# Filler work dealt out at two rates beside the RWKV chunks, and an earlier place for the first feed-forward norm

## The chip, the cores and the metric

The kernel runs on one core of a Trainium2 chip. The metric is the device time of one execution in microseconds, taken as the median of several runs. The core has five instruction queues that matter here: TensorE (PE, with its weight loads shown apart as PEld), VectorE (DVE), ScalarE (ACT), GpSimd (POOL) and SyncE (SP, which issues most DMAs). Each queue is worked off in the order in which it was written, so an instruction that waits holds up everything behind it on its engine.

## What is computed

Two layers on one sequence of 1024 tokens with 1024 channels: an RWKV-7 time mixing layer and an mLSTM layer, each followed by a SwiGLU feed-forward layer, each with a modulated RMS norm ahead. The change touches the first layer's mixing and the start of its feed-forward layer.

```python
h = _rms(x) * (1.0 + sc1) + sh1
y = _rwkv7_mix(h, ...)      # six projections of token-shifted inputs, then per head (16 heads of 64):
#   state = state * w_t + (state @ a_t) b_t^T + v_t k_t^T ;  y_t = state @ r_t   (a scan over time)
#   group norm, bonus, gate g, then  @ w_out
x = x + g1 * y
h = _rms(x) * (1.0 + sc2) + sh2
x = x + g2 * _swiglu(h, w_gu, w_down)     # (silu(h @ w_g) * (h @ w_u)) @ w_down
```

## The kernel before, in words

Channels lie on the 128 partitions and tokens on the free axis. The 1024 tokens are worked in two halves of 512 (`hf` 0 and 1). Every float32 matmul of a projection is made of three fast ones (high part times high part and the two mixed terms), so an output tile of 128 channels by 512 tokens from 1024 input channels is 24 matmuls of 512 columns into a PSUM tile named `dn`.

The RWKV scan is done in blocks: a block is one pair of heads (index `j`, 0 to 7) in one half, 16 blocks in all, and a block holds eight chunks of 64 tokens. Each block goes through five stages, and `chunks` runs them as a pipeline over steps `i` from 0 to 18:

- `rw_prep` (block `i`): decays, masked products within a chunk (`sc`, `c1` from `KB`, `AR`), transposes.
- `rw_inverse` (block `i-1`): the inverse of a triangular matrix per chunk, 30 small DVE operations in a row (L676, L678), DMA round trips through DRAM, then small matmuls into `iv`.
- `rw_solve` (block `i-2`): small matmuls into `px` and `tr`.
- `rw_chain` (block `i-3`): the recurrence itself, eight dependent rounds, each PE, then DVE, then PE, then DVE (matmuls named `c<-st,AR`, `c<-VU,SR`, `c<-VU,KT`; DVE L787, L796; ACT L797).
- `rw_finish` (block `i-3`): group norm (ACT L809, L814), transposes `tr<-kc,Ys`, gate, and a store into `yd`.

Beside the blocks stands the filler, a generator (`fillers`) of work that the blocks don't wait for at once: the projections still missing (v of the first half, the gate, then all of the second half: two low-rank ones, k, r, v, gate), then the output projection of the first half (`project`, into the residual tiles `x0`), then the norm of the feed-forward layer on `x0` (`rstd`, `norm_blocks`, and a split of each tile in high and low part), then five calls of `first`, which do part of the feed-forward layer on the first half (48 matmuls of 512 columns each, weights `wgu`). Ahead of each group of projections `mixed` makes the token-shifted input: eight times two ACT and two DVE operations on 128x512.

Each piece yields how much PE work it was, in units of about five matmuls. `chunks` calls `run(limit)` between the stages of a step, and `run` lets the filler go on until its sum reaches the limit, 16 units per step (`QUOTA`). `until` pulls filler ahead when a block needs a projection that isn't made yet. The output projection can't start until eight blocks are finished (`self.finished < 8`).

The order in which this Python code is written is a priority; a scheduler in the language's layer makes the queues' orders from it, by the priorities and by when it thinks that inputs are there. `self.ahead(part)` gives what is recorded inside it a priority that many instructions earlier (`AHEAD`: chain 50, mask 400, finish 50 and so on).

After the last step `phase(FROOM)` closes the block's buffers, and `ffn` begins with `second`: the output projection of the second half (matmuls `c<-ga,wq`, whose inputs `ga` are splits of the loaded `yd` of that half, so the last block must be finished), and splits of the normed first half (`gb<-x`).

## Time and profile before

| | |
|---|---|
| median of 3 runs | 2932.73 us (2917.15 to 2933.27) |
| the profiled execution, its own time | 2919.56 us |
| its span, first to last instruction | 2917.8 us |
| PE busy | 2702.9 us (93%) |
| DVE busy | 2036.1 us (70%) |
| ACT busy | 1401.1 us (48%) |
| mean granted TensorE clock | 0.949 |
| first recurrence (block 0) to start of the feed-forward layer | 267.9 to 1025.8 us |

The span is read in stages by the program's names. A block's turn is taken here from its first `c<-st,AR` matmul to that of the next block; those starts are at 267.9, 318.6, 369.9, 433.8, 479.4, 516.4, 569.0, 610.0, 653.8, 715.5, 754.1, 793.6, 846.4, 883.0, 928.5 and 976.7 us, and the first `c<-ga,wq` is at 1025.8 us. PE's busy share counts pipelined matmuls by their whole length, so that a stretch of small matmuls also looks busy.

### The profile page before, as it was taken

To read this page: it belongs to the slowest core of one execution; us is meant where nothing else is said; L and a number is where in the kernel's file an instruction comes from. 1 tells how busy PE (TensorE), PEld (TensorE's weight loads), DVE (VectorE), ACT (ScalarE), POOL (GpSimd) and SP (SyncE) were. 2 spreads that over 40 slices of the span, in tenths; PEclk is the share of its full clock that TensorE was granted. 3 is DMA by queue.
4 is the path that set the end of the run, shared out by engine and by line. 5 is a ranking of instruction groups with operands and counts; after the bars stand their busy time and mean duration, and the time that the engine had idled before them with its cause. 6 is when DMAs were issued, how large, how long until landed. Compare 5 with 4: busy or idle time off the path is not lost.

```text
span 2917.8 us, 46574 instructions
## 1 busy us (share of the span) xinstructions
PE 2702.9 (93%) x17080; PEld 2124.4 (73%) x17080; DVE 2036.1 (70%) x4029; ACT 1401.1 (48%) x2641; POOL 74.5 (3%) x98
## 2 busy tenths in 40 slices
PE   6899889999898999999999989999989999999988
PEld 5576556677676677887777767778867788887776
DVE  7877776877676468788877677665556865667645
ACT  5766786777666554322244354233435433323433
POOL 0000000000000000000000000000000000000000
PEclk9899789999798999999999989889989999999999
DMA  8775444455543455577788744345264322347734
GB/s 293 262 266 149 121 128 125 119 158 145 155 138 102 134 199 163 187 228 233 243 276 258 229 138 129 121 152 159 94 205 146 106 100 94 107 138 246 237 118 150
DMA packets 359721, 492.38 MB, mean 169 GB/s; under 512 B 125212, under 2 KB 208796, under 8 KB 359492
## 3 DMA queue, kind: packets, MB, share of 16 engines
q1 hardware_dynamic: 345668, 464.24, 50.1%
q10 hardware_dynamic: 13824, 25.17, 2.4%
q8 instruction: 134, 2.20, 0.3%
q14 instruction: 95, 0.78, 0.1%
HBM read 359.77 MB, written 129.50 MB: 168 GB/s over the span
## 4 chain that ended last, share of the span: by engine, by line
PE 61%; DVE 14%; DMA 11%; ACT 6%; issue 6%; POOL 1%; SPq 1%; DVEq 0%; POOLq 0%; ACTq 0%
PE dn L207 23%; PE c L207 20%; PE iv L207 7%; PE px L207 7%; PE sc L207 2%; DMA wraw<-wsd 2%; DMA tt<-gd 1%; DMA wraw<-in_wdn 1%; DVE wq L212 1%; DMA bgs<-in_ada 1%; DVE ga L212 1%; ACT wq L211 1%; DVE wlo L212 1%; PE tr L207 1%; ACT whi L211 1%
## 5 line engine op out<-in xcount | busy, mean ns | idle before, releaser
L207 PE MATMUL dn<-a,whi 128*128 128x512 f32 (+1 forms) x1200 | 434.4, 428 | 20.4 <-ACT a L211 8.0
L211 ACT ACTIVATE wq<-wraw 128x1024 fp32r<-128x1024 f32 x202 | 210.7, 1057 | 335.4 <-DVE wraw L889 89.6
L207 PE MATMUL c<-ga,wq 128*128 128x512 f32 x1446 | 354.2, 394 | 8.6 <-ACT ga L211 7.8
L207 PEld LDWEIGHTS c<-ga,wq 128*128 128x128 f32 x1446 | 271.5, 189 | 73.7 <-ACT ga L211 10.1
L212 DVE TENSOR_TENSOR wq<-wraw,wq 128x1024 fp32r<-128x1024 f32 x202 | 244.3, 1221 | 85.3 <-ACT wq L211 85.1
L207 PEld LDWEIGHTS dn<-a,whi 128*128 128x128 f32 (+1 forms) x1200 | 226.3, 196 | 81.8 <-ACT a L211 10.7
L207 PE MATMUL dn<-a,wlo 128*128 128x512 f32 (+1 forms) x664 | 275.1, 425 | 5.8 <-ACT wlo L443 2.9
L207 PE MATMUL c<-gb,wq 128*128 128x512 f32 x894 | 220.9, 399 | 9.4 <-DVE wq L212 6.4
L207 PEld LDWEIGHTS c<-gb,wq 128*128 128x128 f32 x894 | 169.2, 191 | 49.5 <-DVE wq L212 7.6
L207 PEld LDWEIGHTS dn<-a,wlo 128*128 128x128 f32 (+1 forms) x664 | 128.8, 197 | 37.1 <-issue 4.8
L211 ACT ACTIVATE whi<-wraw 128x1024 fp32r<-128x1024 f32 (+2 forms) x96 | 100.4, 1046 | 113.2 <-PE dn L207 81.9
L212 DVE TENSOR_TENSOR wlo<-wraw,whi 128x1024 fp32r<-128x1024 f32 (+2 forms) x96 | 116.0, 1208 | 45.7 <-ACT whi L211 39.7
L207 PE MATMUL iv<-ga,wq 128*128 128x512 f32 x552 | 136.0, 389 | 0.0
L207 PE MATMUL px<-ga,wq 128*128 128x512 f32 x528 | 128.7, 389 | 0.0
L211 ACT ACTIVATE w<-wraw 128x384 fp32r<-128x384 f32 (+1 forms) x100 | 56.7, 567 | 139.9 <-PE c L207 62.3
L207 PEld LDWEIGHTS iv<-ga,wq 128*128 128x128 f32 x552 | 103.6, 188 | 21.6
L207 PEld LDWEIGHTS px<-ga,wq 128*128 128x128 f32 x528 | 99.1, 188 | 20.7
L207 PE MATMUL dn<-gb,wq 128*128 128x512 f32 x426 | 104.1, 396 | 5.0 <-ACT gb L211 4.7
L207 PE MATMUL iv<-gb,wq 128*128 128x512 f32 x432 | 104.7, 390 | 0.0
L207 PEld LDWEIGHTS dn<-gb,wq 128*128 128x128 f32 x426 | 81.1, 191 | 23.9 <-ACT gb L211 5.3
L207 PE MATMUL c<-ga,w 128*128 128x512 f32 x372 | 93.4, 393 | 1.1 <-DVE ga L212 0.7
L1124 ACT ACTIVATE x<-x 128x512 f32<-128x512 f32 x77 | 48.3, 629 | 95.0 <-DVE x L933 44.9
(607 smaller groups left out, 5643.5 us busy)
## 6 DMA issues: line engine op xcount, KB each, us to landing
wraw<-in_wgu SPq DMA_DIRECT2D x110, 512.0 KB, 3.5
tt<-gd SPq DMA_DIRECT2D x154, 256.0 KB, 4.1
KT<-in_ada SPq DMA_DIRECT2D x40, 512.0 KB, 5.3
gd<-x SPq DMA_DIRECT2D x77, 256.0 KB, 2.0
gd<-tt SPq DMA_DIRECT2D x72, 256.0 KB, 2.1
wraw<-wsd SPq DMA_DIRECT2D x32, 512.0 KB, 4.7
bgs<-in_ada SPq DMA_DIRECT2D x96, 128.0 KB, 3.3
wraw<-in_wdn SPq DMA_DIRECT2D x24, 512.0 KB, 4.4
```

The lines of the kernel that those rows point to most:

```text
L207: return self.nc.tensor.matmul(out, lhsT, rhs, start=start, stop=stop, **kw)
L211: self.nc.scalar.activation(hi, src, AF.Copy)
L212: self.nc.vector.tensor_tensor(lo, src, hi.bitcast(F32), SUB)
L1124: nc.scalar.activation(t, t, AF.Silu)
```

## The change

`QUOTA` becomes two rates: 19.6 units per step up to step 11 and 12.6 after it, so that the sum at the end of step 18 is 316.4 units where it was 304. The filler has 317. And the norm of the first half with its splits is recorded inside `ahead("front")` with 400.

```diff
-QUOTA = 16
+
+QUOTA = 19.6, 12.6
-AHEAD = dict(chain=50, mask=400, w=50, finish=50, pair=100, g=150, norm=500)
+AHEAD = dict(chain=50, mask=400, w=50, finish=50, pair=100, g=150, norm=500, front=400)
...
         self.store(0, x0)
-        self.norm_blocks(x0, 0, self.rstd(x0))
-        hp = []
-        for x in x0:
-            hi, lo = self.a0()
-            self.split(hi, lo, x)
-            hp.append((hi, lo))
+        with self.ahead("front"):
+            self.norm_blocks(x0, 0, self.rstd(x0))
+            hp = []
+            for x in x0:
+                hi, lo = self.a0()
+                self.split(hi, lo, x)
+                hp.append((hi, lo))
...
+        def quota(x):
+            return QUOTA[0] * min(x, 11) + QUOTA[1] * max(x - 11, 0)
...
-            run(QUOTA * (i + POS[0]))
+            run(quota(i + POS[0]))
...
-            run(QUOTA * (i + 1))
+            run(quota(i + 1))
```

No instruction is added or taken away on any engine; the queues' orders change. Counted on PE in both built programs, the filler's matmuls of 512 columns between one block's first recurrence matmul and the next block's are:

| block | 0 | 1 | 2 | 3 | 4 | 5 | 6 | 7 | 8 | 9 | 10 | 11 | 12 | 13 | 14 | 15, to the feed-forward layer |
|---|---|---|---|---|---|---|---|---|---|---|---|---|---|---|---|---|
| before | 68 | 40 | 89 | 71 | 51 | 93 | 72 | 93 | 135 | 68 | 17 | 86 | 63 | 26 | 110 | 130 |
| after | 65 | 116 | 96 | 72 | 96 | 96 | 96 | 96 | 32 | 96 | 49 | 95 | 57 | 87 | 48 | 0 |

Ahead of block 0's recurrence stand 15 more than before.

Three places show it. Line numbers of the changed kernel are one or two higher up to `rw_finish`. The first place is PE around the norm's matmuls (`sc<-kc,mt` sums the squares, `sc<-kc,rs` spreads the result). Before, they stand in block 13's recurrence, with block 14's solve (`tr<-kc,ld`, `px<-VU,SA`) between:

```order
L207 MATMUL c_302_1589<-st_1582,AR_9163 128x128
L207 MATMUL sc_10670<-kc,mt_10647 128x1 x4
L742 MATMUL tr_10566<-kc,ld_10563 128x128 x3
L207 MATMUL c_302_1589<-VU_10024,SR_9175 64x64 x2
L207 MATMUL c_302_1589<-VU_10024,KT_9220 64x64 x2
L742 MATMUL tr_10566<-kc,ld_10563 128x128
L207 MATMUL px_10582<-VU_10565,SA_9795 64x64
L207 MATMUL sc_10678<-kc,rs_10675 128x128
L207 MATMUL c_302_1589<-st_1582,AR_9163 128x128
L207 MATMUL sc_10678<-kc,rs_10675 128x128
```

The next filler matmul comes 30 rows further down, after the inverse and the solve of block 14 and the first round of its recurrence. In the changed kernel the same matmuls stand at the end of block 11's recurrence, right behind the last matmul of the output projection (`dn_9723`):

```order
L208 MATMUL dn_9723<-a_8329,wlo_9720 128x512
L208 MATMUL c_302_1589<-VU_9134,SR_8397 64x64 x2
L208 MATMUL c_302_1589<-VU_9134,KT_8442 64x64 x2
L208 MATMUL c_302_1589<-st_1582,AR_8385 128x128
L208 MATMUL sc_9955<-kc,mt_9932 128x1 x4
L208 MATMUL c_302_1589<-VU_9134,SR_8397 64x64 x2
L208 MATMUL c_302_1589<-VU_9134,KT_8442 64x64 x2
L208 MATMUL sc_9963<-kc,rs_9960 128x128 x4
L208 MATMUL iv_9297<-XN_9284,SA_8937 16x16 x32
L208 MATMUL dn_10022<-a_9984,whi_10018 128x512
```

Two blocks earlier, and with one matmul row of block 12's inverse before the first `first` matmul (`dn_10022`).

The second place is PE at the end of the last block. Before, filler stands between the last transposes (`tr<-kc,Ys`) and 22 more behind them:

```order
L817 MATMUL tr_11522<-kc,Ys_11356 128x128
L207 MATMUL dn_11544<-a_10723,whi_11539 128x512
L207 MATMUL dn_11544<-a_10724,whi_11539 128x512
L207 MATMUL dn_11544<-a_10723,wlo_11540 128x512
L817 MATMUL tr_11522<-kc,Ys_11356 128x128
```

In the changed kernel the last filler matmul stands ahead of block 15's inverse; its solve, recurrence and transposes have none beside them, and `c<-ga,wq` of the feed-forward layer follows the transposes at once:

```order
L208 MATMUL c_302_1589<-VU_11243,SR_10647 64x64 x2
L208 MATMUL c_302_1589<-VU_11243,KT_10692 64x64 x2
L818 MATMUL tr_11599<-kc,Ys_11433 128x128 x4
L208 MATMUL c_1919_11735<-ga_11692,wq_11732 128x512 x3
L208 MATMUL c_1919_11735<-ga_11697,wq_11732 128x512 x3
```

149 filler matmuls stood behind the start of that inverse before, none now. The third place is ACT at the same point. Before, the last block's scaling (`Ys<-Ys`) is followed by the filler's rest, a weight split (`wq`) and splits `gb<-x`, and then the split `ga<-tt` that the first matmul needs:

```order
L814 ACTIVATE Ys_11356<-Ys_11356,gm_11498,gv_11499 128x64 x8
L978 ACTIVATE tmp_11572<-tmp_11572 128x512
L971 ACTIVATE mt_11594<-dn_11580 128x512
L211 ACTIVATE wq_11732<-wraw_11730 128x1024
L211 ACTIVATE gb_11978<-x_9249 128x512
L211 ACTIVATE gb_11981<-x_9251 128x512
L211 ACTIVATE gb_11984<-x_9253 128x512
L211 ACTIVATE gb_11987<-x_9255 128x512
L211 ACTIVATE ga_11692<-tt_11690 128x512
```

Now the eight `gb` splits stand among the squares (`gj`) of the last block's norm, five `wq` splits stand earlier still, and `ga<-tt` comes right behind the scaling:

```order
L810 ACTIVATE gj_11577,gv_11576<-Ys_11433,gm_11575 128x64
L212 ACTIVATE gb_11996<-x_8281 128x512
L810 ACTIVATE gj_11577,gv_11576<-Ys_11433,gm_11575 128x64
L212 ACTIVATE gb_11999<-x_8283 128x512
L810 ACTIVATE gj_11577,gv_11576<-Ys_11433,gm_11575 128x64 x3
L815 ACTIVATE Ys_11433<-Ys_11433,gm_11575,gv_11576 128x64 x8
L212 ACTIVATE ga_11692<-tt_11690 128x512
```

## Rows read from the trace of the kernel before

**Rows 1.** The page: PE's part of section 1, the clock of section 2 (40 slices)

```profile
PE 2702.9 (93%) x17080; PEld 2124.4 (73%) x17080; DVE 2036.1 (70%) x4029; ACT 1401.1 (48%) x2641; POOL 74.5 (3%) x98
PEclk9899789999798999999999989889989999999999
```

**Rows 2.** Busy time in stretches, all instructions; behind the engines: granted clock, DMA share, GB/s

```profile
267.90:1025.80 757.90, 682.27 (x7647) 494.87 (x7646) 541.76 (x1394) 519.62 (x1249) 33.51 (x30) 0.91 0.46 134
267.90:433.80 165.90, 139.07 (x1483) 95.06 (x1482) 125.67 (x325) 129.38 (x277) 3.99 (x5) 0.85 0.44 127
754.10:793.60 39.50, 33.89 (x440) 25.52 (x441) 24.11 (x57) 25.63 (x71) 1.75 (x2) 0.70 0.50 161
846.40:883.00 36.60, 36.27 (x489) 26.92 (x487) 29.05 (x74) 20.53 (x50) 2.12 (x2) 1.00 0.50 134
```

**Rows 3.** Blocks 3 to 15, filler (tile dn) alone: length, PE, PEld, DVE, ACT, clock

```profile
433.80:479.40 45.60, 20.90 (x71) 12.76 (x71) 0.00 (x0) 4.14 (x8) 0.93 0.42 127
479.40:516.40 37.00, 15.28 (x51) 8.73 (x51) 0.00 (x0) 2.64 (x5) 1.00 0.47 131
516.40:569.00 52.60, 29.58 (x94) 16.66 (x93) 0.00 (x0) 2.08 (x4) 0.94 0.40 114
569.00:610.00 41.00, 21.16 (x72) 12.62 (x72) 0.00 (x0) 1.34 (x3) 1.00 0.53 150
610.00:653.80 43.80, 26.63 (x93) 16.14 (x93) 0.00 (x0) 2.34 (x4) 1.00 0.56 162
653.80:715.50 61.70, 36.56 (x135) 24.12 (x135) 0.00 (x0) 3.53 (x6) 1.00 0.51 139
715.50:754.10 38.60, 23.91 (x69) 12.19 (x68) 0.00 (x0) 4.64 (x8) 0.91 0.57 161
754.10:793.60 39.50, 5.79 (x17) 3.02 (x17) 0.00 (x0) 1.17 (x2) 0.70 0.50 161
793.60:846.40 52.80, 26.62 (x87) 15.59 (x86) 2.98 (x4) 0.00 (x0) 0.90 0.46 135
846.40:883.00 36.60, 18.13 (x63) 10.92 (x63) 1.49 (x2) 0.00 (x0) 1.00 0.50 134
883.00:928.50 45.50, 7.57 (x26) 4.66 (x26) 1.48 (x2) 0.00 (x0) 0.77 0.41 118
928.50:976.70 48.20, 33.07 (x110) 20.39 (x110) 2.75 (x4) 2.39 (x4) 0.93 0.35 104
976.70:1026.00 49.30, 35.01 (x131) 23.08 (x130) 4.14 (x6) 3.54 (x6) 0.96 0.42 142
```

**Rows 4.** Timeline of PE: three filler matmuls, start us, length of all, operation

```profile
1016.34 0.39 PE L207 MATMUL dn<-a,wlo 128*128 128x512 f32 x1
1016.57 0.62 PE L207 MATMUL dn<-a,whi 128*128 128x512 f32 x2
1017.02 0.39 PE L207 MATMUL dn<-a,wlo 128*128 128x512 f32 x1
```

**Rows 5.** Timeline of PE: last projection matmul, norm's sums, first `first` matmul

```profile
894.53 0.40 PE L207 MATMUL dn<-a,wlo 128*128 128x512 f32 x1
...
904.67 0.95 PE L207 MATMUL sc<-kc,mt 128*128 128x1 f32 x8
...
930.80 0.79 PE L207 MATMUL dn<-a,whi 128*128 128x512 f32 x1 [0.57 <-ACT a L211]
```

**Rows 6.** Stretches without filler, all instructions, columns as in rows 2

```profile
756.20:780.10 23.90, 19.68 (x271) 14.48 (x269) 15.21 (x34) 15.76 (x50) 1.75 (x2) 0.50 0.40 134
```

**Rows 7.** Timeline of all engines at the end of the last block

```profile
1011.21 0.33 PE L817 MATMUL tr<-kc,Ys 128*128 128x128 f32 x1 [1.50 <-ACT Ys L814]
...
1022.12 1.06 ACT L211 ACTIVATE wq<-wraw 128x1024 fp32r<-128x1024 f32 x1 [5.43 <-DMA wraw<-in_wro]
...
1023.08 2.17 ACT L211 ACTIVATE gb<-x 128x512 fp32r<-128x512 f32 x4
...
1025.82 0.79 PE L207 MATMUL c<-ga,wq 128*128 128x512 f32 x1 [7.05 <-ACT ga L211]
```

More of the change, by code (lines that the diff above doesn't have):

```diff
@@ L1481, in chunks @@
                 self.rw_solve(S[i - 2])
-            run(QUOTA * (i + POS[1]))
+            run(quota(i + POS[1]))
             if 1 <= i < 17:
                 self.rw_inverse(S[i - 1])
-            run(QUOTA * (i + POS[2]))
+            run(quota(i + POS[2]))
             if i < 16:
```

## The prediction

> **What bounds the kernel now.** I read the page first, then the busy times of stretches, then the filler alone block by block, then PE's timeline where the filler stops. PE is busy for 93% of the span [rows 1], but that share says little in the chunk stage, where small matmuls count as busy too. The change touches only the orders of that stage, 267.9 to 1025.8 us. There PE is busy 682.3 of 757.9 us at a mean clock of 0.91, DVE 541.8 (71%) and ACT 519.6 (69%) [rows 2]: no engine is full, each waits for the others in turn. The clock has two levels, 1.2 and 2.4 GHz; a mean of 0.91 means that about 18% of the stage, 136 us, ran at the lower one.
>
> What a block's turn costs shows in the filler rows [rows 3]. Full-rate filler matmuls start 0.23 us apart: from 1016.34 to 1017.02 us are three steps [rows 4]. Five turns are smooth: 72 filler matmuls in 41.0 us, 93 in 43.8, 69 in 38.6, 63 in 36.6, 110 in 48.2. They lie within 1.5 us of one line, 23 us + 0.23 us per matmul (39.6, 44.4, 38.9, 37.5, 48.3). Below some 63 matmuls the line stops: 51 took 37.0 us and 17 took 39.5. So a turn has a floor of about 38 us, set by the block's own rounds over PE, DVE and ACT, and under it filler costs nothing. Five other turns lie above: 71 in 45.6 (+6.3), 94 in 52.6 (+8.0), 135 in 61.7 (+7.7), 87 in 52.8 (+9.8), 26 in 45.5 (+7.5 over the floor), 39 us together. They are turns in which `mixed` or the norm loads ACT and DVE, or the clock was low (0.93, 0.94, 0.90, 0.77).
>
> The first three blocks are another case: 165.9 us [rows 2] for 197 filler matmuls (68 + 40 + 89 in the table), where the line would give 3 x 23 + 197 x 0.23 = 114 us. ACT is busy 129.4 us (78%) and DVE 125.7 (76%) [rows 2]: `mixed` and the low-rank projections load these two there, and PE waits for them.
>
> **The change part by part.** No instruction is added or removed, and no DMA; every term is a move, and the filler counts per block in the table of the section on the change carry the sum.
>
> Start: 15 more filler matmuls ahead of block 0's recurrence, 15 x 0.23 = 3.4 us, so 267.9 becomes 271.3 us.
>
> Blocks 0 and 1: they now take 181 matmuls, nearly the work that three blocks took before (197), and it is the same stretch of filler. DVE then needs 125.7 us less one block's own DVE work. That work is about 24 us: block 10's turn, with 17 filler matmuls, has 24.1 us of DVE and 25.6 of ACT [rows 2]. So DVE needs 101 us and ACT 129.4 - 22 = 107 us (22 between block 10's 25.6 and block 12's 20.5 [rows 2]). At the shares reached before, 76% and 78%, that is 133 and 137 us; at 86 and 90%, the most I would grant, 118. I take 130. The price by the line alone, 38 + 49.7 = 88 us, is the lower bound, if only PE counted.
>
> Blocks 2 to 14 by the line: six turns of 96 matmuls at 45.1 us (270.6), one of 72 (39.6), one of 95 (44.9), one of 87 (43.0), and four at the floor (32, 49, 57, 48 matmuls: 152). Together 550.1 us.
>
> What lies above the line: three sets of `mixed` (for r, v and the gate) remain, at the mean of 7.9 us of the five turns above, 24 us. The norm remains as well. Before, PE had no filler from 894.9 to 930.8 us, 36 us, because `first` waits for the norm [rows 5]; but block 13's recurrence and block 14's inverse and solve ran in it, so that turn was only 7.5 us over the floor. In the changed order the norm's matmuls stand right behind the last projection matmul, and just two rounds of the recurrence and one part of an inverse stand before the first `first` matmul. The chain itself is not shorter than its parts: from the last projection matmul to the first sum it took 9.8 us (894.9 to 904.7), from there to the first `first` matmul 26.1 us [rows 5], with other work between on ACT and DVE. With priority I estimate half of this 36 us, 18 us, of which the little work beside it covers some 10. So the priority makes the gap shorter but also takes its cover away: 8 us over the line, as before. In all 24 + 8 = 32 us; bounds 15 (the low clock does not come back) and 40 (as before).
>
> Block 15's recurrence so starts at 271.3 + 130 + 550.1 + 32 = 983.4 us, where it was 976.7.
>
> The end: before, 131 filler matmuls lay in the 49.3 us from that start to the feed-forward layer [rows 3]. None are left, so their 30 us of PE work are paid for in the sums above. From the start to the first transposes it was 34.5 us (976.7 to 1011.2), and from there 14.6 us to the first `c<-ga,wq` [rows 7]. The recurrence's rounds are dependent and don't get shorter without filler. The eight `gb` splits now stand among the last block's squares on ACT: 8 x 0.54 us = 4.3 us [rows 7], of which some 3 delay the last norm. In return the weight and input splits that stood behind the transposes are done by then, and only the scaling's end, one `ga` split and its DVE half are left: about 3 us instead of 14.6. So the end takes 34.5 + 3 + 3 = 40.5 us (37 to 47), and the feed-forward layer starts at 1023.9 us instead of 1025.8.
>
> The sum is -1.9 us against the profiled execution's 2919.56 us, thus about 2918. The three runs' median is 13 us above that execution, and one of the runs (2917) is below it; the mean of the four is 2925.7. I put the time at 2925.7 - 2 = 2924 and forecast no change that can be measured, which for this kernel means within 1%, 29 us.
>
> A rule weighed against rows: from 756.2 to 780.1 us, with almost no filler, PE ran at a clock of 0.50, though small matmuls kept it busy 19.7 of 23.9 us [rows 6]. That turn took 39.5 us, and block 12's at full clock 36.6 [rows 3], so 24 us at the lower level cost at most 3 us there: the rounds wait for DVE and ACT anyway. The Trainium skill ("TensorE: Matmul & The Clock Gate", sections Terms and HAM oscillation) prices throttled time at half of it and tells that gaps in TensorE's work bring the low clock back. By that rule the same stretch would have cost 12 us, and the sum would come out about 68 us lower if the changed order kept the clock up for all of the 136 us.
>
> **The rivals.**
> *The early blocks take their filler at PE's price.* Then blocks 0 and 1 cost 88 us and not 130, and the time is about 2924 - 42 = 2882 us. For it: neither ACT nor DVE is full there. Against it: the same filler kept them at 78 and 76% for three blocks [rows 2], as high as in engines that work in a fixed order and wait for each other anywhere in this stage. Even half of it would give 2903.
> *The bare end decides, and the kernel gets slower.* The 149 matmuls that stood behind the start of block 15's inverse cost 149 x 0.23 = 34.3 us where they now stand, if the earlier turns have no room under the floor; the end gives back 8.8 us. That is +25 us, about 2950. For it: six turns of 96 matmuls lie well above the floor, where each matmul has its full price. Against it: two long turns with 17 and 26 matmuls [rows 3] had room for some 80. It decides once more than three of the turns 2 to 9 take over 50 us.
> *Even filler keeps the clock up.* The low clock goes with turns of little filler (0.70, 0.77), and most turns over 60 matmuls ran at 0.9 to 1.0 [rows 3]. If the 32 us above the line fall away, and a part of the time in the first blocks (clock 0.85 [rows 2]), the time is 2924 - 32 = 2892, at most 2880. Against it: the longest low stretch lay where nothing waited for PE [rows 6], so it had cost little. By the Trainium skill's rule named above this case would be the likeliest.
> *The priority does nothing.* `first` still waits for the whole norm, and ACT makes its inputs at 1.3 us per three matmuls of 0.7 us. Then nothing is gained or lost by that edit: 2924 all the same.
>
> **How the numbers follow.** Forecast (with the last rival, which has the same time) 0.50, its own range 2908 to 2940 from the bounds 118 and 137 for the first blocks, 15 and 40 above the line, 37 and 47 at the end, which I don't add up in one direction. Early blocks cheaper 0.17, clock kept up 0.13, bare end 0.20. The range reaches to the other cases, 2884 to 2954. Faster by more than 1%, under 2903 against the median, takes most of the two cheaper cases, 0.25; slower by more than 1%, over 2962, only the bare end together with a bad turn or two, 0.07; the rest is 0.68. That is about what a measurement of this kernel can tell from no change.
>
> **What the changed profile would show.** Right: blocks 0 and 1 together 118 to 137 us with ACT and DVE near 80%; turns of 96 matmuls at 44 to 50 us; no turn under 36 us; block 15's start between 970 and 995 us, and the first `c<-ga,wq` 37 to 47 us behind it with PE at the low clock between; the norm's gap in filler half as long. Wrong: blocks 0 and 1 under 110 us, or turns of 96 matmuls over 50 us, or a first `c<-ga,wq` more than 15 us off 1024 us. From there on both kernels run the same orders, and the spans behind that point should agree within a few us.

## The result and the profile after

The changed kernel is slower: 2953.35 us against 2926.97 us (medians of six runs each), ratio 1.0103 (95% interval 1.008 to 1.0126; it is taken over all runs, the medians alone give 1.009). Its profiled execution took 2953.41 us, its span is 2951.6 us (2917.8 before), so 33.8 us have to be found. Some 7 of them are chance: the profiled execution of the kernel before (2919.56 us) is a short one, 7 to 12 us under the medians of that kernel beside all runs here (2926 to 2932 us). Every comparison of traces below has this in it. The page's PE line and clock line, which answer [rows 1]:

```profile
PE 2706.0 (92%) x17080; PEld 2128.7 (72%) x17080; DVE 2037.2 (69%) x4029; ACT 1408.8 (48%) x2645; POOL 72.3 (2%) x98
PEclk9899889999979789999999998998989999999999
```

The work is the same on every engine, within 8 us. The stretches of the chunk stage, against [rows 2] (columns as there): the whole stage, turns 0 and 1, turns 0 to 2, turns 3 to 14, and the end.

```profile
275.50:1047.60 772.10, 675.73 (x7616) 491.61 (x7615) 546.74 (x1392) 529.53 (x1258) 31.41 (x30) 0.90 0.46 133
275.50:411.80 136.30, 110.08 (x1030) 73.75 (x1028) 99.84 (x236) 106.83 (x208) 1.87 (x3) 0.85 0.44 128
275.50:464.80 189.30, 160.17 (x1554) 109.61 (x1553) 132.85 (x323) 141.40 (x303) 5.25 (x6) 0.86 0.43 125
464.80:1008.10 543.30, 498.74 (x5977) 370.93 (x5975) 396.65 (x1032) 371.53 (x906) 23.34 (x23) 0.94 0.49 140
1008.10:1047.60 39.50, 16.82 (x90) 11.07 (x89) 17.24 (x37) 16.59 (x52) 2.81 (x2) 0.50 0.22 75
```

Turns 0 to 2 take 189.3 us instead of 165.9; turns 3 to 14 take 543.3 us, and 542.9 before (433.8 to 976.7); the end takes 39.5 instead of 49.1. The filler alone for the turns that matter (turns 1, 2, 4, 9, 10, 11, 13; columns as in [rows 3], where turns 4 to 13 of before stand):

```profile
327.80:411.80 84.00, 43.93 (x116) 23.24 (x116) 0.00 (x0) 10.91 (x17) 0.82 0.42 124
411.80:464.80 53.00, 28.10 (x96) 17.24 (x96) 0.00 (x0) 4.66 (x8) 0.90 0.40 117
...
508.10:553.50 45.40, 26.73 (x96) 16.88 (x96) 0.00 (x0) 2.82 (x5) 1.00 0.55 157
...
725.10:778.00 52.90, 27.85 (x96) 17.91 (x96) 2.24 (x3) 0.54 (x1) 0.94 0.58 173
778.00:813.40 35.40, 16.65 (x50) 8.82 (x49) 2.25 (x3) 0.00 (x0) 0.95 0.47 120
813.40:883.80 70.40, 30.15 (x95) 18.99 (x95) 2.18 (x3) 1.16 (x2) 0.78 0.32 93
...
919.90:967.50 47.60, 25.64 (x88) 14.96 (x87) 2.03 (x3) 2.40 (x4) 1.00 0.45 132
```

Turn 4 stands for four with 96 matmuls, at 44.6 to 45.9 us. The long ones are turn 1 (84.0 us) and turn 11 (70.4 us), which holds the norm. PE's timeline there, against [rows 5]: last projection matmul, sums, one row of block 12's inverse, first `first` matmul. Below it DVE in the same stretch.

```profile
846.50 0.40 PE L208 MATMUL dn<-a,wlo 128*128 128x512 f32 x1
...
849.73 1.05 PE L208 MATMUL sc<-kc,mt 128*128 128x1 f32 x8 [0.55 <-DVE mt L331]
...
857.72 0.72 PE L208 MATMUL iv<-XN,SA 16*16 16x16 f32 x64 [3.52 <-DVE XN L696]
859.17 0.79 PE L208 MATMUL dn<-a,whi 128*128 128x512 f32 x1 [0.72 <-ACT a L212]
```

```profile
851.65 0.35 DVE L797 SCALAR_TENSOR_TENSOR st<-st,dl,c 128x128 f32<-128x128 f32 x1 [0.67 <-PE c L208]
...
854.24 3.08 DVE L862 TENSOR_TENSOR x<-x,sc 128x512 f32<-128x512 f32 x5 [1.22 <-PE sc L208]
857.23 0.43 DVE L696 STREAM_TRANSPOSE XN<-XD 128x256 f32<-128x256 f32 x1
```

The gap in filler shrank from 36 us to 12.3 us (846.9 to 859.2), as the priority was to do. But the turn is 25.6 us over the prediction's line (23 us + 0.23 us per matmul), twice the gap, so the gap alone doesn't make it. Block 11's last round ends on DVE at 852.0 us (L797). Behind it stand five of the norm's eight operations (L862), and only then the transpose (L696) that block 12's inverse waits for. So the matmuls of this inverse begin only when the recurrence is over: the transpose comes 43.8 us into the turn, and the next recurrence starts 26.6 us behind it; in turns 4 to 7 the same transpose came 11 to 27 us into the turn, beside the recurrence. How much of the 25.6 us this order makes is not shown.

The end, against [rows 7]: PE at the last transposes and the first `c<-ga,wq`, SP and ACT at the loads between.

```profile
1042.79 0.47 PE L818 MATMUL tr<-kc,Ys 128*128 128x128 f32 x1 [10.97 <-ACT Ys L815]
...
1047.24 3.76 SPq L1505 DMA_DIRECT2D ga<-in_xT  x8
1047.60 5.95 PE L208 MATMUL c<-ga,wq 128*128 128x512 f32 x15 [2.34 <-ACT ga L212]
...
1051.10 1.86 SPq L834 DMA_DIRECT2D tt<-yd  x3
1058.10 1.93 ACT L212 ACTIVATE ga<-tt 128x512 fp32r<-128x512 f32 x3 [7.95 <-DMA tt<-yd]
...
1058.79 3.65 PE L208 MATMUL c<-ga,wq 128*128 128x512 f32 x7 [5.23 <-ACT ga L212]
```

PE waits 11.0 us for the last block's scaling; that costs nothing against the kernel before, where filler ran in this time (the first transpose stands 34.7 us behind block 15's start, 34.5 before). It waits 2.3 us at the first `c<-ga,wq`, and 5.2 us more after 15 of them: the last three loads of `yd` stand on SP behind eight loads of `in_xT` that were issued from 1047.24 on. Before, those eight were issued from 1017.1 to 1024.7 us, ahead of the first `c<-ga,wq` at 1025.8, and PE then went through these matmuls with waits under 0.3 us:

```profile
1020.69 2.83 SPq L1500 DMA_DIRECT2D ga<-in_xT  x6
...
1026.86 1.52 SPq L833 DMA_DIRECT2D tt<-yd  x3
...
1026.89 13.62 PE L207 MATMUL c<-ga,wq 128*128 128x512 f32 x47 [0.27 <-DVE ga L212]
```

So the three loads of `yd` start 3.5 us behind the first `c<-ga,wq`, where it was 1.0 us, and they take 7.0 us to land, where it was 5.2. The feed-forward layer's later matmuls `c<-gb,wq` therefore start 53.3 us behind the first `c<-ga,wq`, where it was 47.2 (columns: start, length of all, operation; before, then after):

```profile
1072.99 2.20 PE L207 MATMUL c<-gb,wq 128*128 128x512 f32 x9
```

```profile
1100.87 2.43 PE L208 MATMUL c<-gb,wq 128*128 128x512 f32 x10
```

The sum of the 33.8 us: block 0's start +7.6, turns 0 to 2 +23.3, turns 3 to 14 +0.5, the end -9.7, the start of the feed-forward layer +6.1, all behind it +5.9. That last part varies by itself: 1842.6 to 1857.7 us over the 20 kernels run here, with the kernel before third from below (1844.8). Why block 0 starts 7.6 us later is not shown.

### The profile page after: what moved, and what is told of

Its sections match the earlier page's. It is cut to its first block, busy times and chain, and to the rows that moved or that the text cites. A ratio compares the mean times of both kernels' runs of the same rounds, so it can differ in the third digit from the quotient of the medians.

```text
span 2951.6 us, 46587 instructions
## 1 busy us (share of the span) xinstructions
PE 2706.0 (92%) x17080; PEld 2128.7 (72%) x17080; DVE 2037.2 (69%) x4029; ACT 1408.8 (48%) x2645; POOL 72.3 (2%) x98
## 4 chain that ended last, share of the span: by engine, by line
PE 39%; DMA 9%; DVE 8%; issue 5%; ACT 2%; SPq 1%; POOL 1%; DVEq 0%; POOLq 0%; ACTq 0%
PE c L208 14%; PE dn L208 13%; PE iv L208 6%; PE px L208 4%; DMA wraw<-in_wdn 2%; DMA wraw<-wsd 2%; DMA bgs<-in_ada 2%; DMA tt<-gd 2%; DVE wq L213 1%; PE sc L208 1%; ACT wq L212 1%; DVE ga L213 1%; DMA tt<-yd 1%; DMA wsd<-bgs 0%; DMA bgs<-in_wdn 0%
## 5 line engine op out<-in xcount | busy, mean ns | idle before, releaser
L208 PE MATMUL dn<-a,whi 128*128 128x512 f32 (+1 forms) x1200 | 435.7, 431 | 24.1 <-ACT a L212 12.5
L208 PE MATMUL dn<-a,wlo 128*128 128x512 f32 (+2 forms) x664 | 278.8, 430 | 6.9 <-DVE wlo L478 4.2
L208 PEld LDWEIGHTS c<-gb,wq 128*128 128x128 f32 x894 | 170.6, 193 | 46.1 <-DVE wq L213 7.3
L208 PEld LDWEIGHTS dn<-a,wlo 128*128 128x128 f32 (+2 forms) x664 | 131.3, 200 | 39.6 <-issue 6.5
L208 PEld LDWEIGHTS iv<-gb,wq 128*128 128x128 f32 x432 | 81.3, 188 | 17.3 <-DVE x L934 0.3
```

The costliest lines, as they stand in the source:

```text
L208: return self.nc.tensor.matmul(out, lhsT, rhs, start=start, stop=stop, **kw)
```

## The experiments

All edits are against the changed kernel, but for e5_light_before, which is made from the kernel before; ratios are to the kernel before on the same chip. "Bare end" means that next to no filler is left behind block 15's start; a "covered" end has it.

**Each half of the change alone.** e1_rates keeps the two rates, without the priority:

```diff
-AHEAD = dict(chain=50, mask=400, w=50, finish=50, pair=100, g=150, norm=500, front=400)
+AHEAD = dict(chain=50, mask=400, w=50, finish=50, pair=100, g=150, norm=500)
```

> The two rates alone, the norm at its old priority. The filler counts per block are those of the changed kernel but for blocks 12 and 13 (48 and 96 for 57 and 87), and no filler stands at the end. Theory A (the bare end): the rates cost nearly all, so about 2950 us, as the changed kernel. Theory B (the norm's priority takes the cover off its gap: block 11's turn took 70.4 us where the line gives 44.9): the turn with the norm falls by some 15 us, so about 2938 us.

Measured 1.0049 (1.0029 to 1.0069). That is half of the loss: less than the first theory had forecast, more than the second. Turns 0 to 2 take 192.4 us and the end is bare, as in the changed kernel; the one turn that differs by much is the norm's, 60.9 us instead of 70.4 (turns 13 and 14 differ too, but take 87.7 and 88.2 us together). DVE in that turn of e1_rates:

```profile
851.96 1.87 DVE L862 TENSOR_TENSOR x<-x,sc 128x512 f32<-128x512 f32 x3
...
856.04 0.44 DVE L696 STREAM_TRANSPOSE XN<-XD 128x256 f32<-128x256 f32 x1
```

Here too the norm's operations, all eight, stand ahead of the transpose, which comes 40.9 us into the turn; so that order comes with the rates, not with the priority. What the priority changes here is the cover: without it the gap is 17.7 us long and five of the recurrence's eight rounds begin in it, with it 12.3 us and one round. The 47 filler matmuls ahead of the gap then take 33.5 us instead of 17.7, and the 48 behind it 24.6 instead of 25.4.

e2_front keeps the priority, at 16 units a step; e12_front_again is the same kernel with more rounds:

```diff
-QUOTA = 19.6, 12.6
+QUOTA = 16, 16
```

> One rate of 16 as before, the norm at priority 400. 136 filler matmuls remain behind block 15's start (130 before). Theory A: the end is as before, so no slower than the kernel before; the turns 13 and 14 with 77 and 56 matmuls in place of 26 and 110 save some 8 us by the line, so 2915 to 2927 us. Theory B: the gap of the norm costs 25 us over the line as in the changed kernel's block 11, so about 2940 us.

> The priority of the norm alone with 16 units a step, the same kernel as in an earlier run (which gave 0.9977), with more rounds to narrow the interval. If the priority by itself brings something, the ratio stays at 0.996 to 0.999; if that was chance, it lies at 1.000 to 1.002.

Measured 0.9977 (0.9957 to 0.9997) and 0.9981 (0.9959 to 1.0002): a gain of some 0.2%, which the first of the two intervals sets apart from none and the second doesn't. So the rates make the kernel slower, and the priority adds some 0.5% to it, while at 16 units, where the norm falls into turn 13, it adds nothing. That it is the many filler matmuls in the norm's turn that make the difference is likely and not shown.

**Other rates.** e3_end gives the filler a flat rate, without the priority, that leaves 51 matmuls behind block 15's start. e4_18 has 18 units and then 12.5, with 136 left there; e8_18_old_norm is the same without the priority; e7_front16_15 has 16 and then 15 with the priority, and 145 left.

```diff
-QUOTA = 19.6, 12.6
+QUOTA = 16.65, 16.65    # e3_end, without front
+QUOTA = 18, 12.5        # e4_18; e8_18_old_norm without front
+QUOTA = 16, 15          # e7_front16_15
```

> One rate of 16.65, whose sum at the last step is that of the changed kernel (316), and the norm at its old priority. Blocks 0 and 1 have 56 and 40 matmuls, as few as before; behind block 15's start stand 51 in place of 130. Theory A: the 79 matmuls gone from the end cost 79 x 0.23 = 18 us, less some 5 us by which the end gets shorter, so about 2940 us. Theory C (the 181 matmuls pressed into blocks 0 and 1 are what costs, 10 us and more): about 2927 us, as before.

> Rates 18 and 12.5 (sum 298 in place of 316), the norm at priority 400 as in the changed kernel. 136 matmuls remain behind block 15's start, and only one turn of 2 to 14 has less than 50. Theory A: the end is paid for again, and by the line of 23 us and 0.23 us per matmul the turns 0 to 14 take 605 us where before they take 624, so about 2908 us, faster than both. Theory B: the norm's gap adds 17 us to that, so about 2925 us. Theory C: blocks 0 and 1 with 130 matmuls cost some 5 us over before.

> Rates 18 and 12.5 as in the fourth run (2970 us), but the norm at its old priority; the counts per block are nearly the same (52 and 52 for 57 and 47 at the end). If the priority made the 45 us gap in filler at the norm there, the gap shrinks and the time falls to about 2945 us; if the rate of 18 puts filler in lumps by itself (a 41 us gap in block 4 and 5, far from the norm), it stays at about 2965 us.

> Rates 16 and 15 with the norm at priority 400: 145 filler matmuls behind block 15's start in place of 130, and turns 13 and 14 with 71 and 65 in place of 26 and 110. Theory A: 15 matmuls more are free at the end (3 us) and the even turns save 8 us, about 2918 us, faster than both kernels by little. If the end is already full, about 2925 us.

Measured: e3_end 1.0057 (1.0041 to 1.0073), e4_18 1.0143 (1.0126 to 1.016), e8_18_old_norm 1.0133 (1.0101 to 1.0166), e7_front16_15 0.9985 (0.9968 to 1.0002). e3_end, with nearly the old first blocks (173.6 us) and without the priority, still loses. Its end and its start of the feed-forward layer, to `c<-gb,wq`, take 96.3 us together, as before, so that 79 matmuls less bring nothing there; turns 0 to 14 take 719.6 us instead of 708.8. e4_18 and e8_18_old_norm are the slowest of all, and that with a covered end (2908 to 2925 us had been forecast for e4_18, 2971 came), so a bare end isn't the only way to lose. In e4_18 filler stops for two long stretches (columns as in [rows 3]):

```profile
521.00:562.00 41.00, 0.03 (x1) 0.00 (x0) 0.00 (x0) 1.08 (x2) 0.63 0.44 113
912.00:957.00 45.00, 0.34 (x2) 0.00 (x0) 0.75 (x1) 0.00 (x0) 0.56 0.37 98
```

The second is the norm's gap. What holds the filler back in the first I did not settle.

**Filler left out at the end.** e6_light_after and e5_light_before compute less: three `first` calls take two of their eight input tiles, 108 filler matmuls less. In the changed kernel these stood in turns 13 and 14, in the kernel before behind block 15's start.

```diff
-            self.product(pa, (hi[:, :HT], lo[:, :HT]), hp[:4])
+            few = 1 if l == 0 and n in (2, 3, 4) else 4
+            self.product(pa, (hi[:, :HT], lo[:, :HT]), hp[:few])
...
-            self.product(pb, (hi[:, HT:], lo[:, HT:]), hp[4:])
+            self.product(pb, (hi[:, HT:], lo[:, HT:]), hp[4:4 + few])
```

> The kernel before, with three of the five early `first` calls (n = 2, 3, 4) summing over a quarter of the input channels: 108 filler matmuls are left out, and 103 of them are missing behind block 15's start (27 left of 130). Its result is so not the layer's. Theory A (the end's length is that of the last block's own chain and the feed-forward layer's start, so filler there is free): no change, 2920 to 2932 us. If filler has its price everywhere: 108 x 0.23 = 25 us less, about 2905 us.

> The changed kernel with the same 108 matmuls left out of the same three calls. There they are missing from the turns of blocks 13 and 14 (23 and 1 left of 87 and 48), none from the end, which has none. Theory A: these turns fall to the floor of about 38 us each, 12 us less, and up to 25 us less if the floor is lower: about 2930 to 2940 us against some 2953 us. If the changed kernel's extra time does not come from the filler's place: no change.

Measured 1.0031 (1.0011 to 1.005) and 1.0121 (1.0086 to 1.0155): no gain from less work in either. In e5_light_before the end and the start of the feed-forward layer take 98.5 us together with 103 matmuls less, 96.3 with them: in the kernel before, filler at the end is free. In e6_light_after turns 13 and 14, with 23 matmuls and 1, take 91.6 us; in the changed kernel, with 87 and 48, 88.2. The filler of these two turns alone, columns as in [rows 3]:

```profile
917.50:974.60 57.10, 9.14 (x24) 4.40 (x23) 2.75 (x4) 2.37 (x4) 0.67 0.44 128
974.60:1009.10 34.50, 0.72 (x2) 0.19 (x1) 0.68 (x1) 0.60 (x1) 0.64 0.45 134
```

The granted clock falls to 0.67 and 0.64, where it was 1.00 and 0.83: about 49 us more at the lower level. Two readings remain: the rounds set the length of these turns, or what was saved in matmuls (108 x 0.23 = 25 us) went into the lower clock. The Trainium skill ("TensorE: Matmul & The Clock Gate", sections Terms and HAM oscillation) prices throttled time at half; by this, as an estimate, 24 of the 49 us, which would fit the second. No run here has these turns light and at full clock, so it stays open. For the kernel both mean the same: filler is free in these two turns.

**First blocks or bare end?** The decomposition above pointed to turns 0 to 2. e9_late has the old rate up to step 6 and the changed kernel's sum from step 11 on, so only the bare end and the priority are left of the change; e10_early has the early rate and then falls back to the old line, without the priority, so only the first blocks are left.

```diff
-            return QUOTA[0] * min(x, 11) + QUOTA[1] * max(x - 11, 0)
+            return 16 * x if x < 6 else (96 + (215.6 - 96) / 5 * (x - 6) if x < 11 else 215.6 + 12.6 * (x - 11))      # e9_late
+            return 19.6 * x if x < 6 else (117.6 + (160 - 117.6) / 4 * (x - 6) if x < 10 else 16 * x)                 # e10_early
```

> The changed kernel with another sum of filler by step: 16 units a step up to step 6 as in the kernel before, then faster, so that from step 11 on the sum is the changed kernel's. Filler matmuls per block: 68 40 89 95 72 144 120 120 32 96 52 92 58 96 38, and none behind the start of block 15's inverse; 681 done by the start of block 3's recurrence as before (776 in the changed kernel). Theory 'the price is paid in the first blocks, where ACT and DVE are loaded': block 3's recurrence starts at 434 us (464.8 in the changed kernel), the middle turns stay near 543 us together whatever filler they hold (three of them with 120 to 144 may add up to 15), and the time is 2922 to 2940 us, though the end is as bare as in the changed kernel. Theory 'the bare end decides': the end has no filler, so the start of the feed-forward layer is no earlier than 1045 us and the time stays at 2945 to 2955 us.

> The kernel before (no priority for the norm, 16 units a step at the end) with 19.6 units a step up to step 6 and then fewer until the sum is back on its line at step 10. Filler matmuls per block: 65 116 96 51 88 50 99 65 82 53 13 74 63 90 56, and 136 behind block 15's start (before 130); 776 done by the start of block 3's recurrence, as in the changed kernel. Theory 'the price is paid in the first blocks': block 3's recurrence starts at about 465 us instead of 433.8, the 95 matmuls less in the turns behind it give little back, and the time is 2945 to 2962 us with an end as full as before. Theory 'the bare end decides': the end is that of the kernel before, so the time is within 6 us of it.

Measured: e9_late 1.0117 (1.008 to 1.0153), e10_early 1.0039 (1.0015 to 1.0062). That overturned the theory that the price is paid in the first blocks alone: with them as before, e9_late (2965.6 us) is as slow as the changed kernel, and slower than either theory had forecast for it. The filler alone in turns 0 to 2, turns 3 to 14 and the end (columns as in [rows 3]): before, e9_late, e10_early.

```profile
267.90:433.80 165.90, 73.36 (x198) 37.24 (x197) 0.00 (x0) 19.82 (x32) 0.85 0.44 127
433.80:976.70 542.90, 265.21 (x885) 157.78 (x885) 8.71 (x12) 24.29 (x42) 0.92 0.47 135
976.70:1025.80 49.10, 35.01 (x131) 23.08 (x130) 4.14 (x6) 3.54 (x6) 0.97 0.41 141
```

```profile
266.50:437.50 171.00, 77.79 (x198) 39.62 (x197) 0.00 (x0) 19.48 (x31) 0.79 0.43 123
437.50:1012.20 574.70, 300.49 (x1015) 181.21 (x1015) 12.84 (x18) 28.06 (x48) 0.94 0.48 138
1012.20:1052.30 40.10, 0.00 (x0) 0.00 (x0) 0.00 (x0) 0.00 (x0) 0.50 0.27 89
```

```profile
282.10:474.20 192.10, 98.63 (x278) 54.55 (x277) 0.00 (x0) 24.12 (x39) 0.84 0.42 123
474.20:1005.80 531.60, 246.48 (x785) 141.76 (x784) 8.74 (x12) 19.95 (x34) 0.89 0.46 132
1005.80:1057.80 52.00, 37.30 (x137) 24.13 (x136) 4.14 (x6) 3.59 (x6) 0.97 0.40 135
```

In e9_late the 130 matmuls that the end lost cost 31.8 us in turns 3 to 14, 0.245 us each, and the end gave back 9.0. (Its profiled run is 16 us below its median.) In e10_early turns 0 to 2 cost 26 us more and turns 3 to 14 give back 11. (Its profiled run is 19 us above its median.) So the first blocks alone explain some 11 of the 26 us in the medians, and the end's filler spread over turns 3 to 14, with the priority, can explain all. A bare end with neither the priority nor the early rate was not run; e3_end, with 51 matmuls left, comes nearest and loses 0.6%.

**The price by place.** Three kernels leave 105 filler matmuls out of the changed kernel, with all operations of the other engines kept: in turns 1 and 2 (e13_light_1_2), in turns 5 to 7 (e14_light_5_7), 67 ahead of block 0 and 38 in turn 0 (e15_light_0). In e14_light_5_7 all other turns hold the same filler within one matmul; in e13_light_1_2 turns 10 to 14 divide the same sum in another way (92, 52, 59, 105 and 28 matmuls), and in e15_light_0 some turns differ by up to 6.

```diff
-            self.dense(ps, wt, xs)
+            self.dense(ps, wt, xs[:1] if hf == 1 and arr == "k" and j < 5 else xs)   # e13; e14: "v"; e15: hf == 0, "v", j > 2
```

> The changed kernel with 105 filler matmuls left out of the second half's k projection (five of its eight output tiles take one input tile of eight, so k is not the true one there). Turn 1 then has 53 filler matmuls instead of 116 and turn 2 has 54 instead of 96; all operations on DVE, ACT and the DMAs stay. The turns from 10 on hold the same sum with another division. Theory 'ACT and DVE bind the first blocks': turns 0 to 2 stay at 185 to 189 us and the time is within 6 us of the changed kernel's, a ratio to before of 1.008 to 1.013. Theory 'every filler matmul costs PE's price of 0.23 to 0.24 us there': block 3's recurrence starts 24 us earlier, at about 441 us, and the ratio is 1.000 to 1.004.

> The changed kernel with 105 filler matmuls left out of the second half's v projection (five of its eight output tiles take one input tile of eight, so v is not the true one there). Turns 5, 6 and 7 have 53, 74 and 56 filler matmuls instead of 96 each; all other turns have the same as in the changed kernel. By the prediction's line (23 us and 0.23 us per matmul, floor 38) these turns go from 45 to 38, 40 and 38 us: block 15's recurrence starts 19 us earlier, at 989 us, ratio 1.003 to 1.007. Theory 'the rounds of the blocks set these turns at 45 us whatever the filler': nothing changes, 1.008 to 1.013.

> The changed kernel with 105 filler matmuls left out of the first half's v projection (five of its eight output tiles take one input tile of eight, so v is not the true one there): 67 of them ahead of block 0's recurrence, 38 in turn 0, which keeps 27. Theory 'ACT and DVE bind the first blocks': block 0's recurrence starts up to 15 us earlier, if PE bounds the stretch ahead of it, and turn 0 stays near 52 us. Theory 'PE's price': both together 24 us earlier. If neither, the ratio stays at 1.010.

Measured: 1.0019 (1.0002 to 1.0035), 1.0061 (1.0037 to 1.0085) and 0.9995 (0.9974 to 1.0016). Against the changed kernel's 1.0103 that is some 25, 12 and 32 us. Turn 1 of e13_light_1_2, the filler alone (columns as in [rows 3]) and then all instructions (columns as in [rows 2]), and the filler of turns 5 to 8 of e14_light_5_7:

```profile
332.10:403.70 71.60, 24.38 (x53) 11.82 (x53) 0.00 (x0) 12.22 (x19) 0.76 0.44 131
332.10:403.70 71.60, 53.38 (x480) 32.30 (x480) 51.85 (x113) 59.43 (x123) 1.75 (x2) 0.76 0.44 131
```

```profile
557.80:598.60 40.80, 15.51 (x53) 9.40 (x53) 0.00 (x0) 2.37 (x4) 0.84 0.47 124
598.60:648.90 50.30, 24.26 (x75) 12.99 (x74) 0.00 (x0) 3.56 (x6) 0.90 0.63 176
648.90:688.40 39.50, 16.96 (x57) 8.89 (x56) 0.00 (x0) 1.78 (x3) 0.96 0.58 160
688.40:731.30 42.90, 11.03 (x32) 5.18 (x32) 0.00 (x0) 4.38 (x8) 0.85 0.58 167
```

Turn 1 with 53 matmuls still takes 71.6 us, 34 above the floor. ACT is busy for 59.4 of these us, so at least 21 of the 34 are ACT's work there and not made by matmuls; the granted clock of 0.76 may have its part in the rest. Turns 0 to 2 get 16.6 us shorter (172.6), 0.16 us per matmul left out, neither the full price nor none. Where whole pieces of filler were moved, with their loads, splits and evictions, the price there was 0.29 us (23.3 us for 80). In the middle only 5.2 us came back in turns 5 to 7, and turn 8 got 7.2 us longer; what e14_light_5_7 gained came elsewhere, 6.2 us of it in turn 11, so that its ratio fell into the range forecast, but not by the turns forecast. In e15_light_0 block 0 starts no earlier (283.3 us, 275.5 in the changed kernel): the 67 matmuls ahead of it bring nothing. Its turn 0 is 11.9 us shorter for 38 less, turn 1 7.7 us shorter with the same 116, and turn 11 14.4 us shorter with 91 instead of 95. So what is left out in one turn is partly won in others, and these three kernels give no clean price by place.

**The mirror image, and a version that beats both.** e16_late_first and e17_late_first_13 take filler out of the first blocks into the middle, with the end covered; e11_ramp and e18_ramp_again (the same kernel) leave the first blocks as they were and even out the middle. All have the priority.

```diff
-            return QUOTA[0] * min(x, 11) + QUOTA[1] * max(x - 11, 0)
+            return 12 * x if x < 6 else (72 + (196 - 72) / 6 * (x - 6) if x < 12 else 196 + 15 * (x - 12))   # e16_late_first
+            return 13 * x if x < 5 else (65 + (208 - 65) / 7 * (x - 5) if x < 12 else 208 + 13 * (x - 12))   # e17_late_first_13
+            return 16 * x if x < 5 else (80 + (208 - 80) / 7 * (x - 5) if x < 12 else 208 + 13 * (x - 12))   # e11_ramp
```

> The mirror image of the change, with the norm ahead: 12 units a step up to step 6, then up to 196 at step 12, 15 a step after it. Filler matmuls per block: 35 26 30 70 96 72 120 111 141 68 31 70 67 72 56, and 136 behind block 15's start; 586 done by the start of block 3's recurrence (681 before, 776 in the changed kernel). If the first blocks are the dear place: turns 0 to 2 take 140 to 150 us instead of 165.9, block 3's recurrence starts at 410 to 422 us, the 89 matmuls more in turns 3 to 14 cost 5 to 22 us by the prices measured so far, and the time is 2905 to 2930 us. If what ACT and DVE do for the filler costs the same wherever it stands, the gain by block 3 is given back in full in the turns behind it, and the time is 2926 to 2940 us.

> As the run before, 13 units a step up to step 5, then up to 208 at step 12 and 13 a step after it. Filler matmuls per block: 32 37 32 136 72 96 96 96 109 67 48 104 40 57 51, and 132 behind block 15's start. If the first blocks are the dear place: turns 0 to 2 at 140 to 150 us, turn 3 with 136 at 54 to 66, and the time 2905 to 2930 us. If the cost moves along with the work: 2926 to 2940 us.

> A version that might beat both: the norm ahead as in the changed kernel, 16 units a step up to step 5, then up to 208 at step 12 and 13 a step after it. Filler matmuls per block: 68 40 88 72 96 99 69 103 80 61 52 105 39 58 48, and 134 behind block 15's start. Theory 'first blocks': block 3's recurrence starts at 434 us as before, the end has its cover, and only the long turns (99, 103, 105) cost by the line; the sum over turns is within 5 us of the kernel before, 2920 to 2932 us. Theory 'bare end': the end is covered, so the same. If the norm's turn alone (105 matmuls with the norm in it) costs 25 us as in the changed kernel, it is 2940 to 2950 us.

> The same kernel as in e11_ramp (0.9963 there), for a comparison on the same chip: 0.994 to 0.998 if its gain stands.

Measured: e16_late_first 0.9969 (0.995 to 0.9988), e17_late_first_13 0.998 (0.9966 to 0.9995), e11_ramp 0.9963 (0.9941 to 0.9985), e18_ramp_again 0.9962 (0.9947 to 0.9978). The filler in the three stretches, e16_late_first and then e11_ramp:

```profile
271.80:404.00 132.20, 37.24 (x91) 18.26 (x91) 0.00 (x0) 11.15 (x18) 0.76 0.40 112
404.00:973.70 569.70, 291.64 (x975) 174.17 (x974) 8.75 (x12) 32.64 (x55) 0.94 0.48 138
973.70:1025.40 51.70, 37.36 (x137) 24.18 (x136) 4.14 (x6) 3.58 (x6) 0.97 0.42 137
```

```profile
267.10:434.20 167.10, 73.62 (x197) 37.11 (x196) 0.00 (x0) 19.49 (x31) 0.85 0.44 128
434.20:964.10 529.90, 267.15 (x882) 154.61 (x882) 8.76 (x12) 24.44 (x42) 0.94 0.49 138
964.10:1014.10 50.00, 35.77 (x135) 23.56 (x134) 4.15 (x6) 3.58 (x6) 0.97 0.41 138
```

In e16_late_first turns 0 to 2 are 33.7 us shorter for 106 matmuls less (0.32 each), and turns 3 to 14 are 26.8 us longer for 89 more (0.30 each): at the feed-forward layer it stands where the kernel before does, 1025.4 and 1025.8. So by the traces the cost goes with the work, and the first blocks are hardly a dearer place (e17_late_first_13: 39.9 us won there for 96, 31.2 lost for 87). The medians, 2918.6 and 2922.0 us, lie within 2905 to 2930, the range named for dear first blocks; as the trace of the kernel before is some 10 us under its medians, a difference of that size between the places stays open. e11_ramp holds the same amounts as the kernel before, but no turn with 135 or 17: turns 3 to 14 take 529.9 instead of 542.9 us. Its time is only 0.1 to 0.2% under that of the priority alone, within the intervals, so that evenness brings something by itself is not shown.

**What the runs show together.** The stage from the starts in the traces:

| | end | turns 0 to 14 | filler in them | end and start of the feed-forward layer, to `c<-gb,wq` |
|---|---|---|---|---|
| before | covered | 708.8 us | 1082 | 96.3 us |
| e7, e11, e16, e17, e18 | covered | 696 to 705 | 1065 to 1078 | 95.7 to 98.3 |
| e2, e12 | covered | 716, 711 | 1076 | 98.9, 98.8 |
| e10 | covered | 723.7 | 1061 | 98.2 |
| e4, e8 (long gaps) | covered | 736, 734 | 1063 | 97.9, 98.1 |
| after | bare | 732.6 | 1197 | 92.8 |
| e1 | bare | 724.5 | 1197 | 93.4 |
| e9 | bare | 745.7 | 1212 | 92.5 |
| e3 | 51 left | 719.6 | 1149 | 96.2 |
| e5 (108 left out) | 27 left | 709.8 | 1077 | 98.5 |
| e6 (108 left out) | bare | 733.7 | 1089 | 91.8 |
| e13, e14, e15 (105 left out) | bare | 709.5, 722.0, 703.0 | 1092, 1092, 1159 | 93.8, 93.4, 92.0 |

A trace is one execution, and some lie off their kernel's median: e10 by +19 us, e2 by +18, e12 by +9, e9 by -16, e5 by -12. In turns 0 to 2 of e2, e12 and e9 PE and DVE work in the same order as before, and yet they take 175.6, 178.2 and 171.0 us instead of 165.9. So in the third column differences up to some 12 us mean nothing by themselves; the 189 to 192 us of these turns in after, e1, e6, e10 and e14 lie outside.

The last column decides: behind block 15's start 130 matmuls more or less change some 4 us (96.3 before; 91.8 to 93.8 with a bare end). Ahead of it, in after, e1 and e9, they cost 16 to 37 us against the kernel before, by where and how evenly they lie.

## Why the prediction was wrong

No change was forecast, 2924 us; 2953 is the edge of the range (2954).

**Where it held.** Blocks 0 and 1 took 136.3 us (130 forecast, 118 to 137), and by the mechanism named: ACT is busy 106.8 us there, 78% (forecast 107 us at 78%), and DVE 99.8 us, 73% (101 us at 76%). The turns of 96 matmuls that lie outside the norm and `mixed` took 44.6 to 45.9 us, as the line says. The end took 39.5 us (40.5 forecast), with PE's granted clock at 0.50. The gap of filler at the norm got shorter by more than half. The floor was set a little high: turns 8, 10 and 12 took 35.7, 35.4 and 36.1 us, against 38 and "no turn under 36 us".

**Where it failed.** The sum missed the start of the feed-forward layer by 23.7 us (1047.6 for 1023.9), and by its terms: the start by 4.2, blocks 0 and 1 by 6.3, blocks 2 to 14 with what lies above the line by 14.2, the end by -1.0. The failing step is the 32 us above the line (15 to 40); measured are 46. Of these 25.6 are the norm's turn alone, to which 8 were given. I priced the norm by PE's gap in filler, 18 us of which 10 would be covered. The gap came out shorter, at 12.3 us, and the turn longer, so the gap was the wrong measure. In place of it the traces show a norm's turn 12 to 26 us over the line (or over the floor of 38 us) in 18 of the 20 kernels, with and without the priority, with gaps from 12 to 59 us, though in some a part is only shifted, as the next turn is short (28.8 us in e11_ramp); only the kernel before (7.5), from which I took the 8, and e3_end (6.2) lie lower. Without the priority it is 16 us (e1_rates, 60.9 us); the other 9.5 us go with the rounds that the priority moved out of the gap, and they are no fixed price: with the priority and 91 to 96 filler matmuls the norm's turn took 56.0 us in e15_light_0, 61.8 in e9_late, 64.2 in e14_light_5_7 and 70.0 in e6_light_after. What makes it so long stays open. The norm's own DVE operations stand ahead of the next block's inverse in the changed kernel and in e1_rates, and behind it in the kernel before; but they stand behind it in e14_light_5_7 too (transpose at 847.3 us, the norm from 853.5), and that turn is still 19 us over the line. Two turns with 96, blocks 2 and 9, lie 7.9 above the line each. For the start, 15 matmuls cost 7.6 us and not 3.4; in e1, e10 and e13, with as many ahead of it, block 0 starts at 274.2, 282.1 and 279.0 us, and with 67 fewer even at 283.3 (e15_light_0), so this is not the price of matmuls, and what it is stays open.

A second step failed behind the end: "the spans behind that point should agree within a few us". I took the feed-forward layer's start as fixed. It lost 6.1 us, 5.2 of them in the wait for the last `yd` loads, which now start behind the input loads that had been issued under the filler. All ends with few or no filler matmuls show it: 51.9 to 56.4 us from `c<-ga,wq` to `c<-gb,wq` in e1, e3, e5, e6, e9, e13, e14 and e15, and 46.1 to 47.2 us in every covered one.

**The rivals.** "The bare end decides" gave about 2950 us, and 2953 came. Its price was 34.3 us for the filler less 8.8 at the end; measured are 31.4 us at block 15's start less 9.7, and e9_late shows the mechanism at 0.245 us per matmul, with the priority beside it. That the number fits so well is partly luck: of the 31.4 us, 7.6 are block 0's later start, which is not the matmuls' price, and a part goes with the norm; 6.1 us at the start of the feed-forward layer were not in this rival's sum. The point from which I let it decide (more than three of turns 2 to 9 over 50 us) was wrong: only turns 2 and 9 are, since most of the price was paid in turns 0 to 2. And the argument against it, room in the turns with 17 and 26 matmuls, was only half of the picture. Those two took 93 more (49 and 87) and got 2 us shorter together; the free room was there and was used. But 80 matmuls went into turns 0 to 2, where nothing was free, and turn 9 went from 38.6 to 52.9 us for 28. "The early blocks take filler at PE's price" is refuted by blocks 0 and 1 themselves, 136.3 us and not 88, and by turn 1, which stays 34 us over the floor with 53 matmuls (e13_light_1_2). "Even filler keeps the clock up" didn't come: by the rows 2 x 0.10 x 772.1 = 154 us of the chunk stage were at the lower level, 136 before. Where the filler was made even with a covered end (e11_ramp) it is 117 us, worked out in the same way from its three stretches, and the time is 0.4% less; how much of that is the clock's, no run tells. "The priority does nothing" is wrong with the two rates, where it costs some 0.5%; at 16 units it gains some 0.2%, hardly clear of nothing.

## What to carry to other kernels

Before filler is moved out of a tail, ask what the tail gets shorter by: if dependent rounds set its length, its filler was nearly free, and it has to be paid for in every turn that is already longer than its own rounds. Price a moved piece with its loads, splits and evictions, not by its matmuls alone, and look for room in the empty turns rather than raise a rate. Price a chain that goes before other work by what waits for it on each engine, not by the gap that it leaves on one. A tail without filler also bares the waits at the start of the stage that follows, so the sum must run on to the first point where both kernels stand alike.

## What was unexpected of the hardware

Leaving 108 matmuls out of turns 13 and 14 made the first 9.5 us longer, the second 6.1 us shorter, and TensorE's granted clock fell from 1.00 and 0.83 to 0.67 and 0.64 there; from 997.5 to 1052.1 us the changed kernel ran at 0.50 throughout:

```profile
997.50:1052.10 54.60, 27.36 (x226) 19.85 (x227) 24.95 (x47) 28.62 (x81) 3.27 (x2) 0.50 0.32 104
```

Less work on this engine was not less time in these two turns. The same order of work can take another time from run to run: turn 1, with the same 40 filler matmuls, took 51.3 us at a granted clock of 0.80 before and 54.0 us at 0.66 in e2_front, e9_late and e12_front_again. And three loads that were issued 2.5 us later against the matmuls that need them, behind eight others in one queue, made PE wait 5.2 us: the DMA engines were busy 88% of the 7.0 us in which they landed, though the stretch before (1008.1 to 1047.6) has a DMA share of only 0.22.
